# The second group's input weights: the rounded part by a casting transfer instead of ScalarE

## The chip, the core and the metric

The kernel runs on one core of a Trainium2 chip. The core's engines run side by side, each through its own list of instructions, in order: TensorE (PE, matrix products), VectorE (DVE), ScalarE (ACT), GpSimd (POOL) and SyncE (SP, which here only issues transfers). They wait for each other by semaphores. Sixteen DMA engines move data between the chip's memory (HBM) and the core's on-chip memory. The metric is the time of one execution on the device in microseconds (us): the median of several runs.

## The reference

One layer of an encoder over two groups of tokens, 1024 and 256 rows of 2048 features, 1280 rows in all. `hn = rms_norm(x, g)`; `proj = hn @ w_in`, whose columns are the inputs of three parts; the layer's result is `x + concat(o_ssd, o_att, o_mem) @ w_out`.

```
hn = rms_norm(x, norm_g);  proj = hn @ w_in
xbc, z_ssd, dt_raw, q, k, v, z_att, mq, z_mem = split_cols(proj, IN_SIZES)
o_ssd:  convolution, silu, two chunked state-space scans (forward, backward), gate, norm     (1024 columns)
o_att:  attention over a window of 128 with ALiBi, 8 heads on 2 key heads, gate              (512)
o_mem:  cross-attention on 256 memory rows, 4 heads, gate                                    (512)
y = x + concat(o_ssd, o_att, o_mem) @ w_out
```

All is float32. Most of the arithmetic is in the products with `w_in` and `w_out`.

## The kernel before

**Products in two parts.** TensorE multiplies a reduced float32 (F32R). So each operand is split into a rounded part H and a rest L = value − H, and a product is the sum of three: H·H, H·L and L·H. For the weights this is `wsplit` (L204 to L208): ACT copies the raw block `wraw` into the F32R tile `wh`, which rounds it (L206), and DVE subtracts `wh` from `wraw` into `wl` (L207).

**Blocks.** The 1280 rows are two groups of five tiles of 128 rows. Weights stream through the core in blocks of 128 input features by 512 columns (256 KB; 288 columns for kv), sixteen to a product. `block_tok` (L234) makes products with tokens on the partitions: for each weight block five token tiles, three matmuls each (L258, L259, L260). `block_feat` (L268) makes them with features on the partitions, from blocks that hold 2 × 256 columns: 24 matmuls a block (L293, L294, L295). `block_pair` makes paired products of seven terms, for the first group's inputs and for half of the output.

**Places.** All weight tiles live in the pool `wp`: four places for `wraw`, three for `wh`, three for `wl`, each 128 × 512 words. A load waits until the subtraction that read its place has been done, a rounding waits until PE has read the `wh` that was there.

**Stages,** by the trace: memory keys and values and the first group's q (to 149 us), the first group's paired inputs (to 496), the first group's kv and z1 (to 591), then the second group's input blocks: x (six `block_feat`, to 820), kv (to 869), q (to 942), za (to 1010), z0, z1 and mq (to 1236) and zm (to 1321); then two output column blocks per half by `block_tok` (name "o", to 1581) and the paired rest.

**What sets the order.** Beside the blocks runs small work: convolutions, attention tiles (`attn`), memory attention (`mem_attn`), the scans (`ssd_up`, `ssd_down`), gates. It stands in two lanes of generators, and after each weight block `pump` takes as many steps from them as a table of rates says (RATES). A step is issued after the instructions in `marks`, the last weight block's rounding and subtraction. The weight splits are written with a raised priority (offset HP[2] = 100). The framework's scheduler then makes each engine's list from priorities and dependencies. Every load and store here is issued by SP, in its order.

**Small work that the prediction names.** An attention tile loads q, DVE makes sums of squares, POOL raises them to the power −1/2 (L123, L124: qr), DVE scales, ACT rounds (qh), PE turns it (pq), ACT copies it back rounded (qT, L673), PE multiplies with the keys (psc, L689), DVE and ACT make the softmax (lg), POOL sets one column (MEMSET lgw, L635) and PE turns it (ppt). `so` (L1060) is the scaled output of a scan, turned by PE (pr). `mpr` is memory attention's softmax.

Of the kernel before, what the change touches and what calls it, by code (L numbers as in the profile page):

```python
# [10 lines left out]
F32 = mybir.dt.float32  # L11
# [8 lines left out]
P = 128  # L20
# [5 lines left out]
HP = (30, 100, 100)  # L26
MR = ((1.9, 0), (1.9, 0))
SCR = 1024
CH, WB, RB, WA, WBB = 4, 3, 4, 5, 4
RBB = 4  # L30

RATES = ({'kv': (4.0, 1.0), 'z1': (2.2, 1.7)},
# [12 lines left out]
def hymba_encoder_kernel(  # L45
# [158 lines left out]
    def wsplit(raw, h, l):  # L204

        a = A.activation(h, raw, AF.Copy)  # L206
        b = V.tensor_sub(l, raw, h.bitcast(F32))  # L207
        marks[:] = a.ins, b.ins  # L208

    def w_laid(src, n):  # L210

        def load(k, raw):
            S.dma_start(raw, src[k])
        return load, n

    def laid_in(name):
        o, n, tok_ = W_AT[name]
# [13 lines left out]
    TURNED = [4 * q + m for q in (0, 2, 1, 3) for m in range(4)]  # L231
    PAIRED = [k + 8 * i for k in range(8) for i in range(2)]

    def block_tok(w, nt, evac, before_last=None, feats=range(KT), places=range(KT)):  # L234

        load, n = w
        ps = [acc.tile([P, 512], F32, tag="acc", name="acc") for _ in range(nt)]
        hls = {}
        for k in range(KT):
            raw = wp.tile([P, 512], F32, tag="wraw", name="wraw", bufs=RB)  # L240
            load(feats[k], raw[:, :n])
            with tc.high_priority(offset=HP[2]):
                h = wp.tile([P, 512], F32R, tag="wh", name="wh", bufs=WB)
                l = wp.tile([P, 512], F32R, tag="wl", name="wl", bufs=WB)
                wsplit(raw[:, :n], h[:, :n], l[:, :n])
            hls[k] = h, l
            if k == KT - 2:
                continue
            if k == KT - 1 and before_last is not None:
                before_last(k)  # L250

            for t in range(nt):
                for k_ in ((k - 1, k) if k == KT - 1 else (k,)):
                    q, m = divmod(places[k_], 4)
                    h, l = hls[k_]
                    sh = cur["H", q][:, m, t * P:(t + 1) * P]
                    sl = cur["L", q][:, m, t * P:(t + 1) * P]
                    T.matmul(ps[t][:, :n], sh, h[:, :n], start=(k_ == 0), stop=False)  # L258
                    T.matmul(ps[t][:, :n], sh, l[:, :n], start=False, stop=False)  # L259
                    T.matmul(ps[t][:, :n], sl, h[:, :n], start=False, stop=(k_ == KT - 1))  # L260
                if k == KT - 1:
                    with tc.high_priority(offset=HP[0]):
                        evac(t, ps[t])
            if k == KT - 1:
                yield k - 1
            yield k

    def block_feat(name, evac):  # L268

        ps = [[acc.tile([P, 512], F32, tag="acc", name="acc") for _ in range(2)] for _ in range(2)]  # L270
        src = laid_in(name)
        hls = {}
        for kk in range(KT // 2):
            raw = wp.tile([P, 512], F32, tag="wraw", name="wraw", bufs=RB)
            S.dma_start(raw, src[kk])
            with tc.high_priority(offset=HP[2]):
                h = wp.tile([P, 2, 256], F32R, tag="wh", name="wh", bufs=WB)
                l = wp.tile([P, 2, 256], F32R, tag="wl", name="wl", bufs=WB)
                wsplit(raw, h.rearrange("p a c -> p (a c)"), l.rearrange("p a c -> p (a c)"))
            hls[kk] = h, l  # L280
            if kk == KT // 2 - 2:
                continue
            tail = kk == KT // 2 - 1

            for kks in ([(kk - 1, kk)] if tail else [(kk,)]):
                for f in range(2):
                    for k in [2 * x + j for x in kks for j in range(2)]:
                        q, m = divmod(k, 4)
                        sh, sl = [x[:, k % 2, f * P:(f + 1) * P] for x in hls[k // 2]]
                        for half in range(2):  # L290
                            c = slice(half * 320, half * 320 + 320)
                            o = ps[f][half][:, :320]
                            T.matmul(o, sh, cur["H", q][:, m, c], start=(k == 0), stop=False)  # L293
                            T.matmul(o, sh, cur["L", q][:, m, c], start=False, stop=False)  # L294
                            T.matmul(o, sl, cur["H", q][:, m, c], start=False, stop=(k == KT - 1))  # L295
                    if tail and f == 0:
                        with tc.high_priority(offset=HP[1]):
                            evac(0, ps[0])
            for k in range(2 * kks[0], 2 * kk + 2):
                yield k  # L300
        with tc.high_priority(offset=HP[1]):
            evac(1, ps[1])
# [40 lines left out]
    def some_left():  # L343
        with ExitStack() as st:
            for ins in marks:
                st.enter_context(tc.issue_after(ins))
            left.popleft()()
# [891 lines left out]
    def weight_sums(src, i):  # L1239

        if i >= 8 * src.shape[0]:
            return
        if i == 0 and src is w_in_pairs:
            raw = fin.tile([P, 512], F32, tag="xst", name="wraw0")
        elif i == 1 and src is w_in_pairs:
            raw = ev.tile([P, 512], F32, tag="evt", name="wraw1")
        else:
            raw = wp.tile([P, 512], F32, tag="wraw", name="wraw", bufs=RB)
        S.dma_start(raw, src[i // 8, i % 8])
        with tc.high_priority(offset=HP[2]):  # L1250
            sums = fin.tile([P, 384], F32, tag="ws", name="ws", bufs=3)
            w11, w12, w22, w21 = [raw[:, i * P:(i + 1) * P] for i in range(4)]
            s1, s2, s4 = [sums[:, i * P:(i + 1) * P] for i in range(3)]
            for o, x, y, op in ((s1, w21, w22, ALU.add), (w21, w11, w21, ALU.subtract),
                                (s2, s1, w11, ALU.subtract), (s4, w12, s2, ALU.subtract)):
                G.tensor_tensor(out=o, in0=x, in1=y, op=op)  # L1256
        ahead.append((raw, sums))

    def block_pair(src, u, rows_of, begin, lead=1):

        ps = {p: (acc.tile([P, 512], F32, tag="acc", name="acc") if i < 5 else psum("accm"))[:, :320]
              for i, p in enumerate(seven)}
        parts, last_split = {}, list(marks)
        for k in range(8):
            weight_sums(src, 8 * u + k + lead)
            with tc.high_priority(offset=HP[2]):
                raw, sums = ahead.pop(0)
                h = [wp.tile([P, 512], F32R, tag="wh", name="wh", bufs=WB),
                     fin.tile([P, 384], F32R, tag="sh", name="sh", bufs=3)]
                l = [wp.tile([P, 512], F32R, tag="wl", name="wl", bufs=WB),  # L1270
                     fin.tile([P, 384], F32R, tag="sl", name="sl", bufs=3)]
                with ExitStack() as st:
                    if u == 0 and k > 1 and src is w_in_pairs:
                        for ins in last_split:
                            st.enter_context(tc.issue_after(ins))
                    wsplit(raw, h[0], l[0])
                    wsplit(sums, h[1], l[1])
            parts[k] = h, l
            if k == 2:
                evac = begin(u)  # L1280
            if k == 6:
                continue
            ks = (6, 7) if k == 7 else (k,)
            for p, (i, m, c) in seven.items():
                for k_ in ks:
                    h, l = [x[i][:, m * P:(m + 1) * P] for x in parts[k_]]
                    xh, xl = rows_of(k_, p, c)
                    T.matmul(ps[p], h, xh, start=(k_ == 0), stop=False)  # L1288
                    T.matmul(ps[p], h, xl, start=False, stop=False)  # L1289
                    T.matmul(ps[p], l, xh, start=False, stop=(k_ == 7))  # L1290
                if k == 7:
                    with tc.high_priority(offset=HP[2]):
                        evac(p, ps[p])
            yield k
# [279 lines left out]
    run(block_tok(w_mem_rows(1), 4, ev_mv, places=TURNED), MR[1], extra=p_step)  # L1574

    def tok(name, w, evac, after=None, grp=0):
        run(block_tok(w, 5, evac), RATES[grp][name], after)

    def feat(name, b, evac, grp, after=None, extra=None):
        run(block_feat(f"{name}{b}", evac), [r / 2 for r in RATES[grp][name]], after, lag=3, extra=extra)  # L1580
# [83 lines left out]

    need(attn, range(4))
    kv_shift()
    run(block_tok(w_kv, 5, ev_dtkv(5)), RATES[1]["kv"], extra=lambda k: some_left() if left else None)
    queue(0, k_prep, range(5, 10))
    queue(0, attn, [4])
    queue(1, dt_prep, [5])  # L1670
    run(block_tok(w_in_rows("q"), 5, ev_raw(q_d, 5)), RATES[1]["q"], extra=when_done(2, lambda: queue(1, ssd_up, range(4, 8))))
    gate("za", 0)
    queue(0, attn, range(5, 10))
    tok("z0", w_in_rows("z0"), ev_gate(0, 5), grp=1)
# [106 lines left out]
```

## Time and profile before

| | us |
|---|---|
| median of 3 runs | 1779.43 (1779.38 to 1779.74) |
| the profiled execution's own time | 1784.13 |
| its span in the profile | 1782.4 |
| the stretch from 591 to 1321 us: PE busy of 730 | 723.2 |
| the same: DVE, ACT, POOL busy | 510.5, 418.3, 69.7 |

The profiled execution took 4.7 us longer than the median of the runs; durations are taken from it, and differences carried over. PE's matmuls are pipelined, so that neighbouring ones overlap in the profile; an idle time of PE is one in which none ran. A row of waits has the engine and line that waited, what ended the wait, the total in us, how often, and the longest. A row of groups has line, engine, operation, tiles written and read, shape, count, then busy us and mean ns of one, then the idle time ahead of them and what ended it.

### The profile page before, as it was taken

Reading aid. Unit: us, or ns where it says so; the run is one execution under the profiler, and the core shown is the slowest. Engines: PE = TensorE matmul, PEld = TensorE weight load, DVE = VectorE, ACT = ScalarE, POOL = GpSimd, SP = SyncE. Lnnn points to the kernel's source line nnn. Section 1 sums busy time; section 2 is a strip of 40 time slices with the busy share of each in tenths; the row PEclk is TensorE's granted clock in tenths of the full one; section 3 lists DMA queues with packets and bytes.
Section 4 is the critical chain, followed back from the end, with each engine's and each line's share of the span. In section 5 each row is a group of like instructions: output and inputs, shape, how many; then the busy total and the mean of one; then the engine's idle time right before and its main releaser. Section 6 shows DMA issues by size and latency. Waiting matters only on the chain. (4 is left out here: it accounts for less than half of the span.)

```text
span 1782.4 us, 31990 instructions
## 1 busy us (share of the span) xinstructions
PE 1766.5 (99%) x11046; PEld 1610.4 (90%) x11046; DVE 1247.7 (70%) x2348; ACT 919.5 (52%) x2049; POOL 554.6 (31%) x980
## 2 busy tenths in 40 slices
PE   9999999999999999999999999999999999999999
PEld 7888999999998999999889988887988888899999
DVE  5595788888868878777765675557777654766665
ACT  5554555554434766666455565645447533533333
POOL 0105798999810100001000100011110000058775
PEclk9999999999999999999999999999999999999999
DMA  9553444445446644553545655557777764644442
GB/s 303 189 183 114 146 149 145 144 141 169 123 145 202 191 136 131 150 168 98 182 121 187 181 160 160 165 170 246 220 244 236 247 191 145 220 142 148 148 142 78
DMA packets 208210, 301.16 MB, mean 169 GB/s; under 512 B 19568, under 2 KB 86192, under 8 KB 208048
## 3 DMA queue, kind: packets, MB, share of 16 engines
q1 hardware_dynamic: 207904, 299.06, 54.6%
q8 instruction: 87, 1.43, 0.3%
q14 instruction: 75, 0.61, 0.1%
q10 hardware_dynamic: 144, 0.06, 0.0%
HBM read 236.36 MB, written 62.69 MB: 168 GB/s over the span
## 5 line engine op out<-in xcount | busy, mean ns | idle before, releaser
L207 DVE TENSOR_TENSOR wl<-wraw,wh 128x512 fp32r<-128x512 f32 (+1 forms) x480 | 347.2, 725 | 229.4 <-ACT wh L206 212.5
L206 ACT ACTIVATE wh<-wraw 128x512 fp32r<-128x512 f32 (+1 forms) x480 | 292.1, 613 | 291.8 <-PE acc L260 156.1
L258 PE MATMUL acc<-wh,xH 128*128 128x512 f32 (+1 forms) x1088 | 418.9, 385 | 0.4 <-DVE v_all L337 0.4
L259 PE MATMUL acc<-wl,xH 128*128 128x512 f32 (+1 forms) x1088 | 410.4, 377 | 0.2
L260 PE MATMUL acc<-wh,xL 128*128 128x512 f32 (+1 forms) x1088 | 410.6, 378 | 0.0
L258 PEld LDWEIGHTS acc<-wh,xH 128*128 128x128 f32 x1088 | 204.6, 188 | 37.3 <-issue 2.7
L260 PEld LDWEIGHTS acc<-wh,xL 128*128 128x128 f32 x1088 | 204.8, 188 | 36.7 <-issue 0.2
L259 PEld LDWEIGHTS acc<-wl,xH 128*128 128x128 f32 x1088 | 204.9, 188 | 36.3 <-DVE wl L207 1.5
L293 PE MATMUL acc<-xH,wh 128*128 128x320 f32 x640 | 202.5, 316 | 0.6 <-DVE zs L309 0.6
L206 ACT ACTIVATE sh<-ws 128x384 fp32r<-128x384 f32 x176 | 91.5, 523 | 210.6 <-POOL ws L1256 111.1
L295 PE MATMUL acc<-xH,wl 128*128 128x320 f32 x640 | 199.1, 311 | 0.0
L294 PE MATMUL acc<-xL,wh 128*128 128x320 f32 x640 | 198.1, 310 | 0.0
L207 DVE TENSOR_TENSOR sl<-ws,sh 128x384 fp32r<-128x384 f32 x176 | 124.9, 713 | 97.0 <-ACT sh L206 94.7
L1256 POOL TENSOR_TENSOR ws<-wraw 128x128 f32<-128x128 f32 x176 | 112.8, 641 | 205.9 <-DMA wraw<-in_w_in_pairs_dram 93.7
L293 PEld LDWEIGHTS acc<-xH,wh 128*128 128x128 f32 x640 | 120.2, 188 | 3.6 <-issue 2.4
L1256 POOL TENSOR_TENSOR ws<-wraw,ws 128x128 f32<-128x128 f32 x176 | 117.9, 670 | 13.8
L294 PEld LDWEIGHTS acc<-xL,wh 128*128 128x128 f32 x640 | 120.2, 188 | 1.3 <-issue 1.0
L295 PEld LDWEIGHTS acc<-xH,wl 128*128 128x128 f32 x640 | 120.2, 188 | 0.7 <-issue 0.7
L1256 POOL TENSOR_TENSOR ws<-ws,wraw 128x128 f32<-128x128 f32 x176 | 117.1, 665 | 0.0
L1256 POOL TENSOR_TENSOR wraw<-wraw 128x128 f32<-128x128 f32 x176 | 111.4, 633 | 13.7
L635 POOL MEMSET lgw<- 128x1 f32 x40 | 3.9, 98 | 310.4 <-DVE lg L698 202.4
L362 DVE SCALAR_TENSOR_TENSOR c<-u,vec,c 128x638 f32<-128x638 f32 (+1 forms) x96 | 90.1, 940 | 9.0 <-ACT c L357 8.7
(440 smaller groups left out, 3957.5 us busy)
## 6 DMA issues: line engine op xcount, KB each, us to landing
wraw<-in_w_in_laid_dram SPq DMA_DIRECT2D x176, 256.0 KB, 2.9
wraw<-in_w_in_pairs_dram SPq DMA_DIRECT2D x112, 256.0 KB, 2.7
wraw<-in_w_out_laid_dram SPq DMA_DIRECT2D x64, 256.0 KB, 3.2
wraw<-in_w_out_pairs_dram SPq DMA_DIRECT2D x64, 256.0 KB, 2.7
rf<-ac SPq DMA_DIRECT2D x40, 256.0 KB, 3.9
rb<-ac SPq DMA_DIRECT2D x40, 256.0 KB, 4.9
wraw<-in_w_mem_laid_dram SPq DMA_DIRECT2D x32, 256.0 KB, 4.7
xst<-in_x_sample_dram SPq DMA_DIRECT2D x20, 256.0 KB, 5.0
```

The lines of the kernel that those rows point to most:

```text
L206: a = A.activation(h, raw, AF.Copy)
L207: b = V.tensor_sub(l, raw, h.bitcast(F32))
L258: T.matmul(ps[t][:, :n], sh, h[:, :n], start=(k_ == 0), stop=False)
L259: T.matmul(ps[t][:, :n], sh, l[:, :n], start=False, stop=False)
L260: T.matmul(ps[t][:, :n], sl, h[:, :n], start=False, stop=(k_ == KT - 1))
L293: T.matmul(o, sh, cur["H", q][:, m, c], start=(k == 0), stop=False)
L294: T.matmul(o, sh, cur["L", q][:, m, c], start=False, stop=False)
L295: T.matmul(o, sl, cur["H", q][:, m, c], start=False, stop=(k == KT - 1))
L362: V.scalar_tensor_tensor(out=c[0], in0=u[:, k:k + n], scalar=cw[k], in1=c[0], op0=ALU.mult, op1=ALU.add)
L635: G.memset(w.bitcast(F32)[(slice(None),) + tuple(slice(n - 1, n) for n in shape)], 0.0)
L1256: G.tensor_tensor(out=o, in0=x, in1=y, op=op)
```

## The change

For the second group's input blocks (x, kv, q, za, z0, z1, mq, zm; 160 weight blocks), `split_loaded` takes the place of `wsplit`: SP loads the raw block as before, and POOL issues a second transfer of the same block from HBM into the F32R tile `wh`, which casts, that is rounds, on the way. DVE's subtraction stays. The other blocks still go by ACT (`split_here`, `block_pair`). The pool's ten places are now named one by one: blocks split by ACT use 4 raw, 3 `wh`, 3 `wl`; the others 2 raw, 5 `wh`, 3 `wl` of the same ten. `marks` holds the subtraction alone for such a block.

```diff
--- before.py
+++ after.py
@@ -26,7 +26,7 @@
-CH, WB, RB, WA, WBB = 4, 3, 4, 5, 4
+CH, WA, WBB = 4, 5, 4
@@ -207,11 +207,40 @@
+    PLACES = {"wraw": deque(range(4)), "wh": deque(range(4, 7)), "wl": deque(range(7, 10)),
+              "lraw": deque(range(2)), "lh": deque(range(2, 7))}
+
+    def wt(kind, name, dtype=F32):
+
+        i = PLACES[kind][0]
+        PLACES[kind].rotate(-1)
+        return wp.tile([P, 512], dtype, tag=f"w{i}", name=name, bufs=1)
+
+    def split_loaded(src, n):
+
+        raw = wt("lraw", "wraw")
+        S.dma_start(raw[:, :n], src)
+        with tc.high_priority(offset=HP[2]):
+            h = wt("lh", "wh", F32R)
+            l = wt("wl", "wl", F32R)
+            G.dma_start(h[:, :n], src)
+            b = V.tensor_sub(l[:, :n], raw[:, :n], h[:, :n].bitcast(F32))
+        marks[:] = [b.ins]
+        return h, l
+
+    def split_here(src, n):
+
+        raw = wt("wraw", "wraw")
+        S.dma_start(raw[:, :n], src)
+        with tc.high_priority(offset=HP[2]):
+            h = wt("wh", "wh", F32R)
+            l = wt("wl", "wl", F32R)
+            wsplit(raw[:, :n], h[:, :n], l[:, :n])
+        return h, l
+
...
@@ -231,19 +260,13 @@
-    def block_tok(w, nt, evac, before_last=None, feats=range(KT), places=range(KT)):
+    def block_tok(w, nt, evac, before_last=None, feats=range(KT), places=range(KT), split=split_here):
...
-            raw = wp.tile([P, 512], F32, tag="wraw", name="wraw", bufs=RB)
-            load(feats[k], raw[:, :n])
-            with tc.high_priority(offset=HP[2]):
-                h = wp.tile([P, 512], F32R, tag="wh", name="wh", bufs=WB)
-                l = wp.tile([P, 512], F32R, tag="wl", name="wl", bufs=WB)
-                wsplit(raw[:, :n], h[:, :n], l[:, :n])
-            hls[k] = h, l
+            hls[k] = split(src[feats[k]], n)
@@ -271,13 +294,7 @@
-            raw = wp.tile([P, 512], F32, tag="wraw", name="wraw", bufs=RB)
-            S.dma_start(raw, src[kk])
-            with tc.high_priority(offset=HP[2]):
-                h = wp.tile([P, 2, 256], F32R, tag="wh", name="wh", bufs=WB)
-                l = wp.tile([P, 2, 256], F32R, tag="wl", name="wl", bufs=WB)
-                wsplit(raw, h.rearrange("p a c -> p (a c)"), l.rearrange("p a c -> p (a c)"))
-            hls[kk] = h, l
+            hls[kk] = [x.rearrange("p (a c) -> p a c", a=2) for x in split_loaded(src[kk], 512)]
...
@@ -1574,7 +1591,7 @@
-        run(block_tok(w, 5, evac), RATES[grp][name], after)
+        run(block_tok(w, 5, evac, split=split_here if name == "o" else split_loaded), RATES[grp][name], after)
@@ -1664,11 +1681,11 @@
-    run(block_tok(w_kv, 5, ev_dtkv(5)), RATES[1]["kv"], extra=lambda k: some_left() if left else None)
+    run(block_tok(w_kv, 5, ev_dtkv(5), split=split_loaded), RATES[1]["kv"], extra=lambda k: some_left() if left else None)
...
```

The scheduler makes a new order from this. Line numbers after the change are higher by 17 in what follows (L673 becomes L690); L226 is the casting transfer, L222 the raw block's load.

ACT, behind the second attention tile that runs beside the x blocks. Before:

```order
L992 ACTIVATE yo<-py 128x512 x2
L365 ACTIVATE u<-c 128x646
L206 ACTIVATE wh<-wraw 128x512
L673 ACTIVATE qT<-pq 128x512
L206 ACTIVATE wh<-wraw 128x512
L673 ACTIVATE qT<-pq 128x512
```

and after:

```order
L1009 ACTIVATE yo<-py 128x512 x2
L988 ACTIVATE rb<-rb,wj_all 128x128
L382 ACTIVATE u<-c 128x646
L988 ACTIVATE rb<-rb,wj_all 128x128 x3
L690 ACTIVATE qT<-pq 128x512
L988 ACTIVATE rb<-rb,wj_all 128x128 x7
L690 ACTIVATE qT<-pq 128x512
```

The two roundings ahead of and between the copies qT are gone; scalings of the scan's decays (L988, before L971) stand there.

POOL, the first two attention tiles beside the x blocks. Before:

```order
L683 COPY lg<-nsink 128x2
L123 TENSOR_SCALAR qr<-qss 128x8
L124 TENSOR_TENSOR qr<-qr,mhalf 128x8
L655 TENSOR_TENSOR qr<-qr,steep 128x8
L635 MEMSET lgw 128x1 x4
L683 COPY lg<-nsink 128x2 x4
```

and after:

```order
L700 COPY lg<-nsink 128x2
L226 DMA wh<-in_w_in_laid_dram 128x512 x2
L123 TENSOR_SCALAR qr<-qss 128x8
L124 TENSOR_TENSOR qr<-qr,mhalf 128x8
L672 TENSOR_TENSOR qr<-qr,steep 128x8
L226 DMA wh<-in_w_in_laid_dram 128x512 x5
L652 MEMSET lgw 128x1
L226 DMA wh<-in_w_in_laid_dram 128x512 x2
L652 MEMSET lgw 128x1
L226 DMA wh<-in_w_in_laid_dram 128x512
L652 MEMSET lgw 128x1 x2
```

Requests of casting transfers now stand between POOL's steps of attention; two ahead of qr, five ahead of the first MEMSET.

SP, around the first two q loads of these tiles. Before:

```order
L275 DMA wraw<-in_w_in_laid_dram 128x512
L490 DMA q<-q_123 128x512
L275 DMA wraw<-in_w_in_laid_dram 128x512
L1000 DMA yp_162<-ya 128x512
L899 DMA rf<-ac_193 128x512
L275 DMA wraw<-in_w_in_laid_dram 128x512 x2
L676 DMA za<-zT_0_118 128x4x128
L275 DMA wraw<-in_w_in_laid_dram 128x512
L490 DMA q<-q_124 128x512
```

and after:

```order
L222 DMA wraw<-in_w_in_laid_dram 128x512
L507 DMA q<-q_123 128x512
L1017 DMA yp_162<-ya 128x512
L916 DMA rf<-ac_193 128x512
L222 DMA wraw<-in_w_in_laid_dram 128x512 x2
L693 DMA za<-zT_0_118 128x4x128
L507 DMA q<-q_124 128x512
```

Between the two q loads stand two raw loads where there were four; each waits for a raw place, of which there are two.

More of the change, by code (lines that the diff above doesn't have):

```diff
@@ L208, in wsplit @@
         marks[:] = a.ins, b.ins
+    PLACES = {"wraw": deque(range(4)), "wh": deque(range(4, 7)), "wl": deque(range(7, 10)),
[22 more added lines that the diff above has]
+        return h, l
     def w_laid(src, n):
-        def load(k, raw):
-            S.dma_start(raw, src[k])
-        return load, n
+        return src, n
     def laid_in(name):
@@ L232, in hymba_encoder_kernel @@
     PAIRED = [k + 8 * i for k in range(8) for i in range(2)]
-    def block_tok(w, nt, evac, before_last=None, feats=range(KT), places=range(KT)):
-        load, n = w
+    def block_tok(w, nt, evac, before_last=None, feats=range(KT), places=range(KT), split=split_here):
+        src, n = w
         ps = [acc.tile([P, 512], F32, tag="acc", name="acc") for _ in range(nt)]
@@ L1247, in weight_sums @@
         else:
-            raw = wp.tile([P, 512], F32, tag="wraw", name="wraw", bufs=RB)
+            raw = wt("wraw", "wraw")
         S.dma_start(raw, src[i // 8, i % 8])
@@ L1267, in block_pair @@
                 raw, sums = ahead.pop(0)
-                h = [wp.tile([P, 512], F32R, tag="wh", name="wh", bufs=WB),
+                h = [wt("wh", "wh", F32R),
                      fin.tile([P, 384], F32R, tag="sh", name="sh", bufs=3)]
-                l = [wp.tile([P, 512], F32R, tag="wl", name="wl", bufs=WB),
+                l = [wt("wl", "wl", F32R),
                      fin.tile([P, 384], F32R, tag="sl", name="sl", bufs=3)]
@@ L1670, in hymba_encoder_kernel @@
     queue(1, dt_prep, [5])
-    run(block_tok(w_in_rows("q"), 5, ev_raw(q_d, 5)), RATES[1]["q"], extra=when_done(2, lambda: queue(1, ssd_up, range(4, 8))))
+    run(block_tok(w_in_rows("q"), 5, ev_raw(q_d, 5), split=split_loaded), RATES[1]["q"], extra=when_done(2, lambda: queue(1, ssd_up, range(4, 8))))
     gate("za", 0)
```

## The prediction

> **What bounds the kernel now.** I read first the page, then the stretch of the second group's input blocks (591 to 1321 us) by windows, then who waits there, engine by engine.
>
> ```profile
> PE 1766.5 (99%) x11046; PEld 1610.4 (90%) x11046; DVE 1247.7 (70%) x2348; ACT 919.5 (52%) x2049; POOL 554.6 (31%) x980
> ...
> 591.00:820.00 229.00, 225.71 (x1702) 216.63 (x1701) 174.72 (x388) 144.19 (x357) 19.05 (x47) 1.00 0.48 144
> 1236.00:1321.00 85.00, 83.51 (x608) 76.06 (x607) 65.67 (x129) 40.34 (x95) 13.21 (x33) 1.00 0.74 229
> sum 730.00, PE 723.20 PEld 649.87 DVE 510.49 ACT 418.33 POOL 69.67; mean PE 120.53 PEld 108.31 DVE 85.08 ACT 69.72 POOL 11.61
> ```
>
> The columns of the lower rows are the stretch, its length, then busy PE, PEld, DVE, ACT and POOL, the granted clock, the DMA engines' share and GB/s. PE sets the time. In the 730 us that the change touches it stands for 730 − 723.20 = 6.8 us; ACT has 312 us free, DVE 219.5. So taking 160 roundings off ACT is worth, first, only what PE waits for ACT, or for DVE behind ACT. PE's waits in this stretch (total, times, longest):
>
> ```profile
> PE psc L689 <- ACT qT L673: 2.5, 1, 2.5
> PE pmt L628 <- DVE mpr L805: 1.5, 1, 1.5
> PE pd L1094 <- DMA ydT<-yd: 0.7, 1, 0.7
> PE acc L293 <- DVE zs L309: 0.6, 1, 0.6
> PE pr L628 <- ACT so L1060: 0.5, 1, 0.5
> PE ppt L628 <- ACT pT L713: 0.3, 1, 0.3
> PE pmo L827 <- ACT mpT L816: 0.3, 1, 0.3
> PE psc L689 <- DVE xs L909: 0.2, 1, 0.2
> ```
>
> No row says that PE waited for a weight part (wh, wl): the weights come in time. All eight are small work (attention, memory attention, scan, gates) that reaches PE late. 5.9 us are ended by ACT or DVE, 0.7 by a transfer.
>
> Two of them can be followed to a rounding, in the timeline of ACT and in the chain of waits:
>
> ```profile
> 680.38 0.73 ACT L365 ACTIVATE u<-c 128x646 f32<-128x646 f32 x1
> 681.02 0.61 ACT L206 ACTIVATE wh<-wraw 128x512 fp32r<-128x512 f32 x1
> 681.54 0.57 ACT L673 ACTIVATE qT<-pq 128x512 fp32r<-128x512 f32 x1
> ...
> 1259.44 0.52 ACT wh L206
> 1259.96 0.49 ACT so L1060
> 1260.50 0.53 PE pr L628 x4
> ```
>
> A rounding (L206) is the row ahead of qT, for which PE waits 2.5 us, and of so, for which it waits 0.5. It costs 0.52 us of ACT's queue, start to start (681.02 to 681.54).
>
> ```profile
> L206 ACT ACTIVATE wh<-wraw 128x512 fp32r<-128x512 f32 x146 | 91.7, 628 | 121.6 <-PE acc L260 56.0 <-PE acc L294 34.2 <-issue 26.5
> DVE wl L207 <- ACT wh L206: 86.6, 59, 5.2
> DVE wl L207 <- DMA wraw<-in_w_in_laid_dram: 5.0, 2, 2.7
> ```
>
> ACT also stands 121.6 us ahead of its roundings, mostly for PE to free one of three wh places, and everything queued behind on ACT stands with it; DVE then stands 86.6 us ahead of its subtraction for the rounding. That standing, more than the 91.7 us of work, makes the small work late.
>
> **The change part by part.** *Removed:* 160 roundings on ACT (48 in x, 16 in kv, 16 in q, 16 in za, 48 in z0, z1, mq, 16 in zm), ACT's waits ahead of them and DVE's for them. The ten wp places are the same bytes, and where a block is still split by ACT they are used 4, 3 and 3 as before, so the rest of the program costs nothing new.
>
> What PE can get back from this: the 5.9 us above. I take all of it, because each is work on ACT or DVE behind queues that lose 213 us of ACT time (91.7 + 121.6) and 86.6 of DVE's. If only the waits with a rounding visible on their chain went, it would be 3.0 (2.5 + 0.5). The other end comes from stalls too short to stand as idle:
>
> ```profile
> L258 PE MATMUL acc<-wh,xH 128*128 128x512 f32 x320 | 130.1, 406 | 0.0
> L293 PE MATMUL acc<-xH,wh 128*128 128x320 f32 x640 | 202.5, 316 | 0.6 <-DVE zs L309 0.6
> ...
> L258 PE MATMUL acc<-wh,xH 128*128 128x512 f32 x202 | 78.7, 390 | 0.0
> L1288 PE MATMUL accm<-tH,wh 128*128 128x320 f32 x216 | 66.8, 309 | 0.0
> ```
>
> The first two rows are this stretch; the third is the first block (10 to 149 us), the fourth the paired blocks (160 to 490 us). The same shapes take 406 against 390 and 316 against 309 ns: 320 × 0.016 + 640 × 0.007 = 9.6 us. As no wait row names a weight, I count none of it; it is the far end of a gain (15.5).
>
> *Added on POOL:* 160 requests of casting transfers in its in-order queue. No POOL request is in this trace. Below, the nearest row is SP's issue of the same block, 0.33 us; above, POOL's dearest small operation, 1.67:
>
> ```profile
> 674.92 0.33 SPq L275 DMA_DIRECT2D wraw<-in_w_in_laid_dram  x1
> L124 POOL TENSOR_TENSOR qr<-qr,mhalf 128x8 f32<-128x8 f32 x10 | 16.7, 1672 | 0.8
> POOL lgw L635 <- DVE lg L698: 202.4, 28, 22.5
> ```
>
> I take 1.0, the middle: 160 us on an engine busy 70 of 730. [...]
>
> Is a weight late behind it? A block comes every 730/160 = 4.56 us. The request for block k waits until PE has read block k−5, so it has four blocks, 18.2 us, for 1.0 of request, the landing, and 0.69 of subtraction. POOL's longest wait, 22.5 us, is longer than that, but the order of instructions puts up to five requests ahead of the waiting MEMSETs, and those after them are for later blocks. I cost this at 0. Behind the waiting request stand POOL's own steps of attention (qr, lgw): they may be late by one request, 1 us, against the 10 to 20 us that POOL stands idle ahead of them; 0 again, and without that cover the attention rival below.
>
> *Added to the transfers:* each block is read twice.
>
> ```profile
> q1 hardware_dynamic: 99591, 122.10, 54.9%
> wraw<-in_w_in_laid_dram SPq DMA_DIRECT2D x139, 256.0 KB, 2.9
> rb<-ac SPq DMA_DIRECT2D x28, 256.0 KB, 4.6
> ```
>
> 122.10 MB took 54.9% of 730 us, so 262144 bytes take 0.86 us of all sixteen engines. 144 whole and 16 narrow copies (147456 bytes) are 40.1 MB, 132 us: the share goes from 55 to 73%, in zm from 74 to 74 + 16 × 0.86/85 = 90%. A transfer with one such copy ahead lands 0.86 later. PE waits for a transfer once (0.7 us, ydT), which becomes 1.6: cost 0.9. Bounds: 0, and what the first rival costs.
>
> *Moved:* raw blocks have two places, not four, so the load of block k leaves after the subtraction of k−2.
>
> ```profile
> SPq L213 <- DVE wl L207: 123.3, 57, 6.1
> SPq L275 <- DVE wl L207: 108.2, 47, 7.5
> ```
>
> SP already stands 104 times for a raw place. From the subtraction of k−2 to that of k there are 9.1 us for a landing of 2.9 (with one copy ahead 3.8): 5.3 to spare, cost 0. Behind SP's wait stand all loads and stores of the small work.
>
> **Sum:** −5.9 + 0 + 0.9 = −5.0 us. The profiled execution took 1784.13 us with a span of 1782.4; it should become 1779.1 with 1777.4. The median of the runs is 1779.43, so 1774.4.
>
> **The rivals.** *Raw blocks late (slower).* With SP held for its longest 7.5 us and a landing as slow as rb's 4.6, a raw block needs 12.1 us and has 9.1: 3.0 late, where four places left 18.2 − 12.1 = 6.1 in hand. DVE stands at the subtraction, and all small work behind it. For: the DMA share of 73 to 90%, and three transfers (wh, raw, the small work's) wanted at the same moment, when PE frees a place. Against: the median 2.9. It decides where DVE's waits for raw blocks pass the 92 us (86.6 + 5.0) that it stands now. At half the blocks, 80 × 3.0 = 240 us, DVE has no time left (219.5 free) and PE waits some 20; halfway between 92 and 240, half of that: 1779.4 + 10 = 1789.
>
> *POOL held long (slower).* If a request only gets on while DVE is idle, which is 219.5/730 = 30% of the time, 1.0 becomes 3.3 us, and POOL is busy 160 × 3.3 + 70 = 598 of 730. The qr steps of ten attention tiles then stand behind up to two requests, 2 × 2.3 = 4.6 us late each. If a quarter of 10 × 4.6 reaches PE, +12: 1791. For it: the order shows requests on both sides of these steps. Against: weights still have 18.2 us. [...]
>
> *Nothing gained.* The small work is late for its own chains on DVE, 70% busy, and the order merely shuffles which wait shows: 1779.
>
> **How the numbers follow.** A difference under 0.2%, 3.6 us, counts as none. The forecast, −5, has 0.48; by its bounds (3.0 less 0.9, and 15.5) it runs from 1764 to 1777, of which 0.45 lies beyond 3.6 us. Nothing gained has 0.20 (0.03 faster, 0.15 same, 0.02 slower), raw blocks late 0.20 (0.01 same), POOL held 0.12. So faster 0.48, same 0.19, slower 0.33. The likeliest's own range is 1766 to 1777; the range for 8 in 10 reaches into both slower rivals, to 1793.
>
> **What would show it.** Right: between 591 and 1321 us no L206 rows on ACT, DVE's wait for wh gone, PE's wait for qT gone, PE's idle time near 2 us, POOL requests near 1 us and PE waiting for no weight. Wrong: DVE waiting at the subtraction for wraw by more than 92 us; POOL requests over 2 us and PE waiting for work behind qr; or the same 6 us of PE waits under other names.

## The result, and the profile after

The changed kernel takes 1828.0 us (median; 1827.1 to 1839.1) against 1779.6 for the kernel before on the same chip: 1.028 of its time, with a 95% interval of 1.026 to 1.030. It is 48 us slower where 5 us faster was forecast. In the changed block code the subtraction is line 227.

From the page of the changed kernel, the span, the engines' busy time and the new queue:

```profile
span 1827.1 us, 31990 instructions
PE 1782.5 (98%) x11046; PEld 1622.9 (89%) x11046; DVE 1249.1 (68%) x2348; ACT 838.0 (46%) x1889; POOL 639.4 (35%) x1140
q0 software_dynamic: 23040, 40.12, 8.2%
```

The span grew by 44.7 us. The work that was to leave ACT has left (919.5 to 838.0 us), and the same PE instructions are 16.0 us longer (1766.5 to 1782.5). The windows of the changed kernel (stretch, its length, busy PE, PEld, DVE, ACT, POOL, granted clock, DMA share, GB/s) show where, for the whole stretch of the second group's input blocks and for two places inside it:

```profile
591.00:1367.00 776.00, 739.08 (x4838) 661.14 (x4836) 511.16 (x1121) 333.71 (x875) 152.03 (x334) 0.98 0.70 209
636.30:643.10 6.80, 5.40 (x21) 5.41 (x22) 2.17 (x9) 4.53 (x14) 0.10 (x1) 0.50 0.25 86
1045.90:1049.30 3.40, 3.40 (x9) 2.63 (x8) 0.69 (x1) 0.00 (x0) 0.53 (x1) 0.50 0.52 169
```

What took 730 us takes 776. PE stands for 776 − 739.08 = 36.9 us of it, where it stood for 6.8: 30 us. The other 15.9 (739.08 − 723.20) goes with a lower granted clock of PE: 0.98 over the stretch, and 0.50 in eight pieces of 3.4 or 6.8 us, two of which are shown. Each begins in a wait of PE or right behind one, so these 16 us are counted here as a price of the waits too; no run sets the clock apart from the waits. The DMA share rose to 0.70, as forecast (0.73).

The waits of the changed kernel in this stretch (total us, times, longest), PE first, then DVE, ACT and POOL:

```profile
PE psc L706 <- ACT qT L690: 11.3, 6, 4.4
PE pmt L645 <- DVE mpr L822: 3.6, 2, 1.9
PE pmo L844 <- ACT mpT L833: 2.8, 2, 1.8
PE acc L310 <- DVE zs L326: 2.6, 1, 2.6
PE psc L706 <- DVE nm L708: 2.1, 1, 2.1
PE acc L281 <- DVE zs L336: 2.0, 1, 2.0
PE pd L1111 <- DMA ydT<-yd: 1.5, 1, 1.5
...
DVE wl L227 <- PE acc L282: 60.9, 36, 5.5
DVE wl L227 <- PE acc L312: 36.0, 20, 4.9
DVE wl L227 <- DMA wraw<-in_w_in_laid_dram: 8.6, 5, 4.0
DVE wl L227 <- DMA wh<-in_w_in_laid_dram: 7.0, 3, 4.3
...
ACT rf L988 <- DMA rf<-ac: 80.7, 28, 5.2
ACT rb L988 <- DMA rb<-ac: 37.7, 17, 4.4
...
POOL wh L226 <- PE acc L312: 175.0, 52, 10.2
POOL wh L226 <- PE acc L283: 96.7, 31, 8.9
```

PE still waits for no weight part. It waits for the same kinds of work as before, in more places and longer; qT alone went from 2.5 to 11.3 us. DVE's 86.6 us of waiting for a rounding are gone and 96.9 us of waiting for PE stand in their place: at the subtraction it is now a place of the second parts that is missing. For the landing of the rounded part itself DVE stands only 7.0 us. ACT, freed of its roundings, stands for the scan's decay rows (rf, rb) instead, 118 us; in the kernel before it stood for rf

```profile
ACT rf L971 <- DMA rf<-ac: 2.6, 2, 1.8
```

and for rb not at all at this step. What stands behind these scalings in ACT's queue is late with them. PE's longest wait, the 4.4 us for qT, ends at 637.70 us; ahead of it ACT does this (start us, us, what, and in brackets the wait before it):

```profile
634.84 2.33 ACT L988 ACTIVATE rb<-rb,wj_all 128x128 f32<-128x128 f32 x7 [3.95 <-DMA rb<-ac]
637.07 0.57 ACT L690 ACTIVATE qT<-pq 128x512 fp32r<-128x512 f32 x1
```

The landings of the changed kernel in the stretch (median us from issue), and its requests by lines (busy us, mean ns, idle before):

```profile
wh<-in_w_in_laid_dram POOLq DMA_DIRECT2D x141, 256.0 KB, 3.9
wraw<-in_w_in_laid_dram SPq DMA_DIRECT2D x141, 256.0 KB, 4.0
rf<-ac SPq DMA_DIRECT2D x29, 256.0 KB, 4.4
...
L226 POOL DMA_DIRECT2D wh<-in_w_in_laid_dram x157 | 85.9, 547 | 389.1 <-PE acc L312 175.0 <-PE acc L283 96.7 <-PE psc L707 26.5
```

and the row of rf in the kernel before (the raw blocks landed in 2.9 us there):

```profile
rf<-ac SPq DMA_DIRECT2D x29, 256.0 KB, 3.6
```

A request holds POOL for 0.55 us, and its data is there 3.9 us after the issue, where ACT's rounding took 0.6. The chain of waits of the changed kernel shows once, in order of time (start us, us), what a late rounded part does:

```profile
1194.52 7.69 issue
1202.22 0.01 POOLq L226
1202.23 6.46 DMA wh<-in_w_in_laid_dram
...
1208.77 0.69 DVE wl L227
1209.46 0.39 DVE lg L708
...
1209.92 0.39 PE psc L706
```

POOL stands 7.69 us ("issue" in the chain; POOL's timeline names PE's L283) until PE has freed a rounded place, the transfer lands 6.46 us later, DVE makes its subtraction, and only then the attention step (lg) that stood behind it, for which PE waits 2.1 us. The weight itself is not late for PE; what stands behind it in DVE's queue is. In the changed kernel this is the only wait of PE with such a chain; the next sections show in which versions it becomes the rule.

### The profile page after: what moved, and what is told of

Same layout as the page of the kernel before. It is cut to its first block, busy times and chain, and to the rows that moved or that the text cites. A ratio compares the mean times of both kernels' runs of the same rounds, so it can differ in the third digit from the quotient of the medians.

```text
span 1827.1 us, 31990 instructions
## 1 busy us (share of the span) xinstructions
PE 1782.5 (98%) x11046; PEld 1622.9 (89%) x11046; DVE 1249.1 (68%) x2348; ACT 838.0 (46%) x1889; POOL 639.4 (35%) x1140
## 5 line engine op out<-in xcount | busy, mean ns | idle before, releaser
L283 PE MATMUL acc<-wh,xL 128*128 128x512 f32 (+1 forms) x1088 | 412.0, 379 | 0.0
L206 ACT ACTIVATE wh<-wraw 128x512 fp32r<-128x512 f32 (+1 forms) x320 | 194.6, 615 | 172.7 <-PE acc L283 95.4
L283 PEld LDWEIGHTS acc<-wh,xL 128*128 128x128 f32 x1088 | 205.6, 189 | 37.0 <-issue 0.2
L226 POOL DMA_DIRECT2D wh<-in_w_in_laid_dram x160 | 87.9, 549 | 401.6 <-PE acc L312 175.0
L311 PE MATMUL acc<-xL,wh 128*128 128x320 f32 x640 | 202.8, 317 | 0.0
```

Of the source, the lines that this page charges most:

```text
L226: G.dma_start(h[:, :n], src)
```

## The experiments

No version leaves out a part of the computation. Times are medians, with the ratio to the kernel before on the same chip and its 95% interval; the kernel before was at 1779.3 to 1780.3 us throughout. "Places 2/5/3" means two raw, five rounded, three second parts for the second group's blocks.

### Places and rounding taken apart

ACT's rounding with the changed kernel's places:

```
-            G.dma_start(h[:, :n], src)
-            b = V.tensor_sub(l[:, :n], raw[:, :n], h[:, :n].bitcast(F32))
+            wsplit(raw[:, :n], h[:, :n], l[:, :n])
```

> The second group's blocks rounded by ACT as before, with nothing read twice and no request on POOL, but with the changed kernel's places: two raw, five rounded, three second parts. Theory P (places): the load of block k waits on SP for the subtraction of k-2, and that for PE to have read k-5, where before it was k-4 and k-7; all of SP's transfers come some 9 us closer to PE's need, and this costs the 48 us. It expects 1810 to 1830. Theory T (transfers): the second reading and POOL's requests make the small work's transfers late (rf landed in 4.4 us, not 3.6, yp in 4.3, not 2.7), and the places cost nothing. It expects 1776 to 1786. Theory D (DVE): with five rounded places it is DVE's subtraction that stands for a place of the second parts (97 us), in its own queue. It expects 1800 to 1825 here too, as the subtraction still stands for three places.

Measured 1798.7, 1.010 (1.008 to 1.013): 19 us, less than theory P asked and more than theory T allowed. The waits of this version:

```profile
ACT wh L206 <- DMA wraw<-in_w_in_laid_dram: 149.7, 95, 6.8
...
SPq L222 <- DVE wl L207: 274.8, 116, 8.6
```

ACT now stands at the rounding for the raw block itself, which SP could ask for only after the subtraction two blocks earlier. So the moved places alone cost 19 us, by making raw blocks late for the engine that consumes them first. DVE stands 81.9 us here for PE to free a second part, with ACT's rounding: most of the changed kernel's 96.9 came with the places, not with the transfers.

Casting transfers with other places, by this line with other numbers (and, in the second and third version, four places of their own for the second parts):

```
-              "lraw": deque(range(2)), "lh": deque(range(2, 7))}
+              "lraw": deque(range(4)), "lh": deque(range(4, 7))}
```

> The casting transfers with the places of the kernel before: four raw, three rounded, three second parts. P expects the time before within 5 us, 1775 to 1785, as the load of block k waits for PE's k-7 again. T expects 1815 to 1830, as all bytes and requests are those of the changed kernel. D expects 1800 to 1825: the request on POOL and the subtraction on DVE both stand for PE's k-3.

> The casting transfers with three raw places, three rounded, four second parts: the load of block k waits for the subtraction of k-3, which waits for PE's k-7. P expects 1775 to 1787, T 1815 to 1830. D expects that DVE's waits for PE at the subtraction fall from 97 us to under 40, since the rounded part's place is now the later one, and 1780 to 1795.

> The casting transfers with two raw places, four rounded, four second parts: the load of block k waits for the subtraction of k-2, which waits for PE's k-6. P expects half of the loss, 1795 to 1810, T 1815 to 1830. D expects DVE's waits for PE at the subtraction to fall under 50 us from 97, and 1785 to 1800.

Measured: 4/3/3 1877.4, 1.054 (1.051 to 1.057); 3/3/4 1876.7, 1.054 (1.052 to 1.057); 2/4/4 1862.9, 1.047 (1.045 to 1.049). All are slower than the changed kernel, and P and D fall: giving the raw blocks or the second parts their places back makes it worse. T's range is passed as well. The waits of the 4/3/3 version say what is missing:

```profile
DVE wl L227 <- DMA wh<-in_w_in_laid_dram: 104.2, 58, 8.6
...
POOL wh L226 <- PE acc L312: 111.3, 30, 10.6
```

DVE stands for the rounded part's landing. This made theory R (the rounded part comes a request and a landing after PE has freed its place) the next to test.

### Bytes, SP's queue, DVE's order

> ACT rounds, places two, five and three, and each of the 160 blocks is read a second time by a request on POOL, but into a spare place in DRAM that nothing reads: the bytes and the requests of the changed kernel, without any work that waits for them. With ACT's rounding and the same places, and no second reading, the kernel took 1798.7 us; the changed one 1828.0. Theory B (bytes): the 40 MB make every landing longer (rf 3.8 to 4.6 us, yp 2.4 to 4.3), and that is the 29 us between the two: 1818 to 1835. Theory R (rounded part late): the bytes cost nothing; a rounded part is now ready 0.5 us of request and 3.9 of landing after PE has freed its place, where ACT made it in 0.6, and DVE's in-order subtraction passes this on: 1796 to 1804.

> The kernel before (ACT rounds, places four, three, three) with each block of the second group read a second time into a spare place in DRAM, by a request on SP right behind the block's load. B expects about 20 to 30 us over the kernel before: 1799 to 1812. R expects 1778 to 1785; SP has 160 more requests of 0.33 us, which its waiting hides.

```
+            G.dma_start(spare_d[0][:, :n], src)
```

(with spare_d in DRAM and ACT's rounding; in the second version on SP, behind the block's load). Measured 1869.2, 1.050 (1.047 to 1.053), and 1810.2, 1.016 (1.014 to 1.019). Neither answers the question. The row of the spare tile in the first of them gives the first and the last request's time:

```profile
L228 POOL DMA_DIRECT2D spare<-in_w_in_laid_dram x160: 486/486/791, 1.3 to 207.6; - x160
```

No work of the layer needed these transfers, so they left in the program's first 208 us (in the second version from 57 to 304) and disturbed the blocks there: in the first of them PE is busy 169.8 of the first 225 us, in the kernel before 221.7. They were repeated with their order fixed, below.

> The changed kernel, with the raw blocks requested on POOL too, so that SP no longer stands for a raw place and the small work's loads and stores leave as soon as they can. Theory S (SP held): SP stands 243 us of the stretch for DVE's subtraction, and with two raw places these waits come 9 us closer to PE; that is the larger part of the loss: 1790 to 1808. B and R expect no gain, 1822 to 1840, R the upper half, since POOL's queue now stands for raw places as well.

```
-        S.dma_start(raw[:, :n], src)
+        G.dma_start(raw[:, :n], src)
```

Measured 1832.2, 1.029 (1.026 to 1.032), the same as the changed kernel (1828.0, 1.028). SP's standing for raw places was not it: theory S falls. (SP then stood for other work in its order, 111.3 us for the scan's state to store, st.)

> The changed kernel without the priority that puts a block's request and subtraction ahead of other work, so that the subtraction stands later in DVE's order. Theory D (DVE stands at the subtraction, 97 us for PE to free a second part): the waits of DVE for PE there fall below 60 us, and the time to 1800 to 1818. B and S expect 1820 to 1835, R slower than the changed kernel, 1835 to 1860, since a late rounded part is asked for later still.

```
-        with tc.high_priority(offset=HP[2]):
+        with tc.high_priority(offset=0):
```

(in the changed blocks only). Measured 1821.2, 1.024 (1.020 to 1.027): 7 us less than the changed kernel, with intervals that just overlap, and short of D's range. DVE still stood 84.9 us for PE there, where D asked for less than 60. R, which expected a slower kernel, misses too. At most a small part lies in DVE's order.

### Second readings inside the stretch, and a small casting request

```
+        with tc.issue_after(a.ins):
+            S.dma_start(spare_d[0][:, :n], src)
```

> ACT rounds, places two, five and three, and behind each block's load SP requests a second reading of the block into a spare place in DRAM. The order of SP's queue is fixed so that each second reading leaves right behind its load, inside the stretch of the second group; in the two runs with second readings before this one nothing held them there, and they had left long before it, at the program's start. Theory B (bytes) expects the changed kernel's time, 1815 to 1835, from 1798.7 without the second reading. Theory R (the rounded part comes late behind PE) expects 1797 to 1806.

> The kernel before, places four, three, three, with the same second readings behind each load. B expects 20 to 30 us over 1779.4: 1799 to 1812. R expects 1778 to 1786.

(a is the block's load.) In both the spare transfers now run through the stretch, as the tile's row of the first shows (576 to 1327 us):

```profile
L226 SPq DMA_DIRECT2D spare<-in_w_in_laid_dram x160: 488/495/1869, 576.2 to 1326.6; - x160
```

Measured: with places 2/5/3 1810.5, 1.019 (1.016 to 1.021), 12 us over the same version without them and between the two theories; with the places of before 1780.7, 1.001 (1.000 to 1.002), hardly to be told from no change, as R said and B did not. And this although, with the places of before, the traffic and the landings are as high as in the changed kernel:

```profile
q1 hardware_dynamic: 119152, 176.46, 69.0%
...
rf<-ac SPq DMA_DIRECT2D x36, 256.0 KB, 4.3
```

So the bytes and the longer landings cost 1.4 us, with an interval that reaches to 0, where loads leave seven blocks ahead (4/3/3), and 12 us where they leave five ahead (2/5/3).

> ACT rounds 480 of a block's 512 columns (256 of 288 in kv), and a casting transfer on POOL the first 32; places two, five and three. So the request on POOL, its wait for PE and the landing behind it are there for every block, DVE's subtraction needs both parts, and the bytes read twice are one sixteenth. R expects most of the 29 us between ACT's rounding (1798.7) and the changed kernel (1828.0): 1812 to 1832. B expects 1797 to 1806.

```
-            wsplit(raw[:, :n], h[:, :n], l[:, :n])
+            G.dma_start(h[:, :32], src[:, :32])
+            a = A.activation(h[:, 32:n], raw[:, 32:n], AF.Copy)
+            b = V.tensor_sub(l[:, :n], raw[:, :n], h[:, :n].bitcast(F32))
```

Measured 1808.6, 1.017 (1.015 to 1.018): 10 us over ACT's rounding with the same places, between the two theories. DVE stood for the landing only 0.9 us in all, so these 10 us are not that wait; what they are was not found. The queue and the landing of this version, whose transfers carry almost nothing:

```profile
q0 software_dynamic: 22608, 2.58, 4.6%
...
wh<-in_w_in_laid_dram POOLq DMA_DIRECT2D x157, 16.0 KB, 2.8
```

> ACT rounds, nothing is read twice, and the second group's places are three raw, four rounded, three second parts, between the kernel before (four, three, three: 1779.4) and two, five, three (1798.7). If the 19 us between those two come from raw blocks that are asked for too late (ACT waited 149.7 us for raw blocks with two places, and seldom with four), a third raw place takes most of it away: 1778 to 1785. If they come from the three places of second parts being the first to fill, so that DVE stands instead of ACT (82 us at the subtraction for PE), they stay: 1790 to 1800.

Measured 1781.4, 1.0015 (1.0006 to 1.0024): the third raw place takes 17 of the 19 us away. ACT's wait for raw blocks went with it:

```profile
ACT wh L206 <- DMA wraw<-in_w_in_laid_dram: 3.8, 3, 2.0
```

### What decides under casting transfers

> As the run with the small casting request (ACT rounds 480 of 512 columns, POOL's transfer brings 32), but with the places of the kernel before: four raw, three rounded, three second parts. Theory R (the rounded part comes a request and a landing after PE has freed its place, and everything behind on DVE with it): with three rounded places that chain has the least cover, so most of the 98 us of the casting transfers with these places: 1830 to 1875. Theory W (two raw places are what costs; requests and bytes cost only on top of them): 1779 to 1788.

Measured 1837.2, 1.032 (1.030 to 1.034): 58 us, from a casting transfer of 16 KB per block, with ACT's work, the bytes and the places all but those of the kernel before. Theory W falls. DVE's waits in this version are those of the casting 4/3/3 version:

```profile
DVE wl L228 <- DMA wh<-in_w_in_laid_dram: 102.5, 49, 8.2
```

This is the cleanest run for R: ACT stands only 9.8 us for rf here, against 80.7 in the changed kernel, so with three rounded places it is the chain of freed place, request and landing that costs.

> ACT rounds, nothing is read twice, two raw, four rounded, four second parts. If the 19 us of two, five, three follow the raw places, they stay: 1795 to 1802, with ACT waiting some 150 us for raw blocks. If they follow the second parts' places, they go: 1779 to 1786.

Measured 1785.4, 1.002 (1.001 to 1.004): 13 of the 19 us are gone with two raw places still there.

```profile
ACT wh L206 <- DMA wraw<-in_w_in_laid_dram: 22.5, 14, 5.1
```

So it is not the raw places by themselves. The load of block k waits for the subtraction of k − raw, and that, for its second part, for PE's block k − raw − second: 7 blocks back with 4/3/3, 6 with 3/4/3 and 2/4/4, 5 with 2/5/3. Under ACT's rounding these cost 0, 2, 6 and 19 us.

> Casting transfers, three raw, four rounded, three second parts. R: the rounded places decide, and with four of them it is like two, four, four (1862.9): 1850 to 1868. W: the third raw place takes back what it took back under ACT's rounding, 17 us or more, from the changed kernel: 1790 to 1815.

> Casting transfers, three raw, five rounded, two second parts. R: the time of the changed kernel or a little more, since the rounded places are the same and DVE now stands for one of two second parts: 1822 to 1845. W: 1795 to 1812, by the third raw place.

Measured: 3/4/3 1839.8, 1.034 (1.030 to 1.038); 3/5/2 1811.5, 1.017 (1.015 to 1.019). The third raw place does not bring the casting version near the kernel before. Both results lie outside R's ranges, on the fast side; 3/5/2 lies inside W's, 3/4/3 far above it.

> Casting transfers, two raw, six rounded, two second parts. Theory R (the rounded part comes late behind PE) expects a further step down from the changed kernel (five rounded places): 1805 to 1822. Theory L (lead of the raw loads: the load of block k waits for the subtraction of k-2 and, by two places of second parts, for PE's k-4, where the changed kernel has k-5 and the kernel before k-7) expects it slower than the changed kernel: 1832 to 1860.

Measured 1813.3, 1.018 (1.016 to 1.020): faster than the changed kernel by 15 us with a lead of only four blocks. Theory L falls here, R's range holds.

> Casting transfers, three raw, five rounded, two second parts (1811.5), and the request and the subtraction without their priority. In the changed kernel this took 7 us off. If DVE's standing at the subtraction delays the small work, the same again: 1800 to 1808. If the gain there came from the two raw places, nothing: 1808 to 1816.

Measured 1810.9, 1.016 (1.014 to 1.018), against 1811.5 with the priority: nothing.

All places side by side, as us over the kernel before:

| raw/rounded/second | 4/3/3 | 3/3/4 | 2/4/4 | 3/4/3 | 2/5/3 | 3/5/2 | 2/6/2 |
|---|---|---|---|---|---|---|---|
| rounded by ACT | 0 | – | 6 | 2 | 19 | – | – |
| casting transfers | 98 | 97 | 84 | 60 | 48 | 32 | 33 |

With casting transfers every place that moves from the second parts to the rounded parts gains: 37 us (3/3/4 to 3/4/3), 35 (2/4/4 to 2/5/3), 28 (3/4/3 to 3/5/2), 15 (2/5/3 to 2/6/2). A place that moves from the second parts to the raw blocks gains too, if less: 23 (2/4/4 to 3/4/3) and 17 (2/5/3 to 3/5/2), which is what W said of the third raw place. In the 3/5/2 version DVE stands even longer for second parts, and the time is the best of the casting versions:

```profile
DVE wl L227 <- PE acc L282: 61.2, 40, 5.5
DVE wl L227 <- PE acc L312: 54.0, 35, 4.9
```

Standing of DVE for PE to free a second part, 115.2 us here and 96.9 in the changed kernel, is therefore not by itself a loss. No version beats the kernel before.

Which lateness reaches PE differs from version to version. In the traces each wait of PE can be followed back, row by row (to what ended it, or to the row ahead in the same queue), until a transfer's landing is met. From 589 to 1400 us, in us:

| version | PE's waits | of these from wh | from wraw | from rf, rb |
|---|---|---|---|---|
| before | 8.3 | 0 | 0 | 1.8 |
| rounded by ACT, 2/5/3 | 20.4 | 0 | 14.3 | 0.2 |
| small request, 2/5/3 | 26.1 | 1.1 | 17.5 | 0.5 |
| small request, 4/3/3 | 41.1 | 21.7 | 1.3 | 0.3 |
| casting, 4/3/3 | 67.7 | 37.7 | 2.6 | 11.9 |
| casting, 2/5/3 (changed kernel) | 37.8 | 2.1 | 1.1 | 24.5 |
| casting, 3/5/2 | 27.4 | 1.8 | 2.8 | 15.0 |
| casting, 2/6/2 | 29.9 | 0 | 3.2 | 19.8 |

So theory R describes the versions with three rounded places. With five, as in the changed kernel, the rounded part is seldom late, and most of PE's waits stand behind ACT's wait for rf and rb. Those rows did not come much later in PE's order; ACT came to them sooner. In the kernel before it scaled them 7.0 us (rf) and 32 us (rb) after their landing, in the changed kernel 0.02 us after it (medians of the stretch). The order shown with the change has this: the scalings L988 stand ahead of qT and between the two qT, where the roundings stood. All versions in which ACT rounds, the small request too, have `marks` hold the rounding; the casting ones do not. No run gives these scalings their old place under casting transfers, so this share is read from the traces and not shown by an experiment.

## Why the prediction was wrong

The sum was −5.9 + 0 + 0.9. Two steps failed: the zero in the middle, for the new requests and the moved places, and the gain of 5.9, which did not come. Measured in the order in which they were tried, the places cost 19 us, the second reading 12 and the small request 10; that makes 41 of the 48. It is an account and no proof that they add: how far each part costs depends on the others, and all three were measured with ACT rounding.

**"What PE can get back from this: the 5.9 us" (removed work): failed.** The rows of the rounding went from ACT, as forecast, but "queues that lose 213 us of ACT time (91.7 + 121.6) and 86.6 of DVE's" was wrong on both engines. DVE's 86.6 came back as 96.9 under another releaser, a missing second part; with ACT's rounding in the same places it is 81.9. ACT's time came back as 118 us of waiting for rf and rb. ACT's freed queue did not do its next work sooner, as that work waited for a landing: ACT came to the scalings of rf and rb before their rows were there, and stood (80.7 and 37.7 us), with qT behind it. PE's wait for qT grew from 2.5 to 11.3 us, and 24.5 of PE's 37.8 us go back to these landings.

**"Cost 0" for two raw places: failed, 19 us.** The 9.1 us from one subtraction to the second next is no slack: the subtraction itself waits for PE, and behind the load stands ACT's rounding, with its own small work behind it. The run without transfers shows this under ACT's rounding only; in the changed kernel DVE waits 8.6 us for raw blocks in all.

**"I cost this at 0" (requests on POOL): failed, 10 us with the changed kernel's places.** The request itself was overpriced (0.55 us, not 1.0; both bounds held). The cover was compared with the 18.2 us until PE needs the weight. But the subtraction is due earlier than that: it stands at a fixed place in DVE's in-order queue, with attention and scan behind it, and those are late as soon as DVE reaches it before the landing. With three rounded places that is most of the loss (58 us for the small request, 98 for the full transfers). With five it held for all but three blocks, 7.0 us of DVE's time, so it is not the larger part of the 48; nor does it explain the 10.

**"+0.9" for the second reading: right for the cause it named, wrong where the lead is short.** Landings did grow by about one copy (rf 3.6 to 4.4), and PE's own wait for ydT became 1.5, forecast 1.6. The term counted only landings for which PE itself waits; those of rf and rb reach it through ACT. Measured alone, with the places of before, the reading is 1.4 us with an interval that reaches to 0; with places 2/5/3 it is 12.

What stays open: what the 32 us at the best casting places are. DVE does not stand there for the rounded part's landing (0 us in 3/5/2 and 2/6/2), so lateness of the rounded part at the subtraction is not it; ACT's 100 us of standing for rf and rb and the second reading are the candidates.

**The rivals.** "Raw blocks late" named the right side and part of the mechanism, and priced it at 10 us; it cost 19 in the run that isolates it. Its condition, DVE waiting for raw blocks by more than 92 us, did not come true, since in that run ACT was the engine that waited and in the changed kernel DVE waited for a second part. "POOL held long" fell: its 3.3 us for a request were a supposition, and requests stay at 0.55 us with DVE busy for 511 of the stretch's 776 us. "Nothing gained" said that "the order merely shuffles which wait shows"; most of PE's waits do lead to the new order now, but they are 37 us and not 6. That the clock could fall behind PE's waits was in no term and no rival, and its 16 us are a third of the loss.

## What to carry to other kernels

When a step is taken off an engine, ask what the engine will reach sooner, and whether that work's operands are there sooner too; in an in-order queue what stands behind it is late with it (here qT behind rf and rb: PE's wait for it went from 2.5 to 11.3 us). When a step is moved to an engine or a queue with a longer latency (here from 0.6 to 3.9 us), measure its cover not to the moment when the last consumer needs the data, but to the moment when the first in-order engine reaches the instruction that waits for it, and name the work behind it there. When places are traded between buffers of one chain, count how many blocks back in the consumer's order each request now waits; a lead that was ample (7 blocks, a second reading for 1.4 us) can be two blocks from one that is not (5 blocks, 12 us). A wait that vanishes may only have covered another: look for the next missing operand before counting it as a gain.

## What the runs showed of the hardware that was not expected

In the changed kernel more comes with PE's waits than their length: the granted clock is 0.50 for 3.4 or 6.8 us in or behind waits of 1.5 to 4.4 us, eight times, and PE's busy time grew by 16 us beside 30 us more of waiting. The row of 1045.90 above follows the wait of 2.0 us for zs; the first row below follows one of 1.9 us, for xs. The kernel before has one such piece, behind its wait of 1.5 us for mpr (the second row). The length of a wait does not decide it alone: in the kernel before, PE's wait of 2.5 us for qT ends inside the third window, whose clock stays at 1.00.

```profile
1008.30:1011.70 3.40, 3.40 (x15) 3.40 (x14) 2.20 (x5) 0.65 (x2) 0.19 (x1) 0.50 0.36 139
...
855.40:858.90 3.50, 3.50 (x17) 3.50 (x17) 0.47 (x2) 1.04 (x3) 0.00 (x0) 0.51 0.83 225
...
681.00:684.50 3.50, 2.34 (x15) 2.34 (x16) 2.58 (x7) 3.02 (x9) 0.00 (x0) 1.00 0.75 236
```

That the lower clock follows from the waits is read from where the eight pieces and the one piece stand; no run tests it.

A casting transfer's landing grew far less than its size: 16 KB landed in 2.8 us in the version with the small request and places 2/5/3, and 256 KB, sixteen times as much, in 3.9 in the changed kernel (medians from issue), with a DMA share of 0.58 there and 0.70 here.

Forty more megabytes in this stretch, which raised the DMA share from 57 to 69%, cost 1.4 us (0 to 3.4) with loads seven blocks ahead, and 12 us with loads five blocks ahead, where the share went from 54 to 67%.
